# Seven half products for eight in the wide part of an in-projection, in two passes over pairs of token blocks

## The chip, the cores and the metric

One core of a Trainium2 chip. The metric is device time in microseconds (us) of one execution of the whole program; lower is better. TensorE (PE) multiplies, with its weight loads listed apart (PEld); VectorE (DVE), ScalarE (ACT) and GpSimd (POOL) do elementwise work; DMAs are issued from two queues, SyncE's (SP) and GpSimd's (POOL).

## The reference, cut to what matters

One layer on 2048 latent tokens (4 blocks of 512) and 256 context tokens, model width 1024, all in float32:

```python
h = rmsnorm(x, norm_g) * (1 + scale) + shift          # 2048 x 1024
ckv, kr, kb, vb, cq, za, qb, zb, ga, gb = split_cols(h @ w_in, ...)
q  = rmsnorm(cq, g_cq) @ w_uq                         # low-rank up-projections
kv = rmsnorm(ckv, g_ckv) @ w_ukv
oa = block_attention(q, k, v)                         # 8 heads, keys: latent and context
ob = neighborhood_attention(qb, kb, vb, ...)          # 8 heads
ya = (oa * silu(za)) @ w_oa;  yb = (ob * silu(zb)) @ w_ob
x  = x + gate * ((sigmoid(ga) * ya + sigmoid(gb) * yb) @ w_out)
out = rmsnorm(x, final_g)
```

The change is in `h @ w_in`, in the columns of qb, za, zb, ga and gb.

## The kernel before, in words

Every float32 product is made of three products of rounded parts: each operand is split into a high part (an ACT copy to the rounded type) and a low part (a DVE subtraction of that copy), and `mm3` multiplies high by high, high by low and low by high into one PSUM bank. So 128 columns of the in-projection (a chunk) for one token block are 8 k-tiles x 3 = 24 matmuls of 128x512 (`chunk`, PSUM tile accm).

Stage one (to about 216 us) computes h, block by block, and splits it into hh0..hh3 and hl0..hl3, 2 MB each, which stay in SBUF; beside it run the narrow columns (kv, q low-rank) and the context. Stage two is a list of items. Chunks 0 to 3 are the neighbourhood keys (evac_k), 4 to 7 its queries (evac_q), 8 to 15 the gates za and zb, 16 to 31 the gates ga and gb (evac_g: ACT sigmoid, for za and zb a DVE product, a store). Chunks 16 and 17 run as fillers elsewhere; the other 26 of chunks 4 to 31 are those that the change regroups. vb runs in two halves of 256 columns (`vb_run`: 16 token tiles x 24 matmuls, tile vacc) whose weights vhi and vlo have one buffer each in the pool vw.

Before each block of chunks 0 to 19, `pump(side_gen, 1)` takes one step of a side generator: first const_gen, then lowrank_gen, the up-projections. One of its steps is 3 matmuls for K (tile ka) or V (va), or 6 for q (qa), then `split_store`: ACT writes the high part into a tile sk or sq of the tag st (two buffers), DVE the low part, and POOL issues the stores to kmS or qm in DRAM (two stores for K and q, eight for the rope part of q, sqr). Its inputs (cnk, cnq) are loaded on SP's queue one block ahead. gate_gen (the output gate, tile pg) and presplit_gen (16 jobs that split w_o and w_out and store the parts) go beside the later chunks.

The attention follows in one loop: for a unit, 20 max matmuls (pm) with a DVE maximum each, a fold and a POOL spread, one matmul that puts the negated maximum in a row (pmf, copied by ACT into qh), then scores (S), exponentials (P) and outputs (oacc).

A scheduler decides from dependencies and priorities what order each engine's instructions stand in; each engine runs its own in order.

## Time and profile before

| | |
|---|---|
| median of 3 runs | 2533.22 us (2532.98 to 2537.31) |
| profiled execution, its own time | 2537.19 us |
| its span in the trace | 2535.4 us |
| TensorE busy | 2489.2 us, 98% |
| DVE, ACT, POOL busy | 1105.9, 903.1, 1093.5 us |
| mean granted clock of TensorE | 0.995 of full |

The span runs from the first to the last instruction of the trace. Busy shares are means over stages with different limits, so a change inside the in-projection has to be read from that stretch, 216 to 1055 us.

### The profile page before, as it was taken

Reading aid. Unit: us, or ns where it says so; the run is one execution under the profiler, and the core shown is the slowest. Engines: PE = TensorE matmul, PEld = TensorE weight load, DVE = VectorE, ACT = ScalarE, POOL = GpSimd, SP = SyncE. Lnnn points to the kernel's source line nnn. Section 1 sums busy time; section 2 is a strip of 40 time slices with the busy share of each in tenths; the row PEclk is TensorE's granted clock in tenths of the full one; section 3 lists DMA queues with packets and bytes.
Section 4 is the critical chain, followed back from the end, with each engine's and each line's share of the span. In section 5 each row is a group of like instructions: output and inputs, shape, how many; then the busy total and the mean of one; then the engine's idle time right before and its main releaser. Section 6 shows DMA issues by size and latency. Waiting matters only on the chain.

```text
span 2535.4 us, 34849 instructions
## 1 busy us (share of the span) xinstructions
PE 2489.2 (98%) x12796; PEld 1833.4 (72%) x12796; DVE 1105.9 (44%) x2285; ACT 903.1 (36%) x1774; POOL 1093.5 (43%) x861
## 2 busy tenths in 40 slices
PE   7999999999999999999999999999999999999998
PEld 4878888877789888756566656565656564888998
DVE  4654221222311211255465545465545446455654
ACT  4664432212322122234444444444444444112221
POOL 1312111111310000268877878777878886133220
PEclk9999999999999999999999999999999999999999
DMA  7535766456652466631415141514150333755542
GB/s 269 191 94 166 253 225 193 126 164 192 191 167 89 121 208 209 177 85 47 100 33 129 39 110 39 121 38 110 39 129 15 76 135 123 262 184 164 179 146 71
DMA packets 182979, 342.86 MB, mean 135 GB/s; under 512 B 25130, under 2 KB 95950, under 8 KB 175438
## 3 DMA queue, kind: packets, MB, share of 16 engines
q1 hardware_dynamic: 168872, 299.01, 39.5%
q0 software_dynamic: 13504, 41.35, 5.8%
q8 instruction: 100, 1.64, 0.3%
q14 instruction: 71, 0.58, 0.1%
q10 hardware_dynamic: 432, 0.28, 0.0%
HBM read 214.42 MB, written 126.13 MB: 134 GB/s over the span
## 4 chain that ended last, share of the span: by engine, by line
PE 89%; DMA 3%; DVE 3%; SPq 1%; ACT 1%; issue 1%; POOL 1%; POOLq 0%; DVEq 0%; ACTq 0%
PE accm L135 26%; PE S L807 15%; PE oacc L807 10%; PE pm L807 6%; PE f L135 5%; PE ya L135 4%; PE vacc L135 4%; PE nacc L226 3%; PE no L807 3%; PE accf L135 2%; PE accx L135 1%; PE nm L807 1%; DMA rz<-rzS 1%; PE pstl L185 1%; PE qa_False L135 1%
## 5 line engine op out<-in xcount | busy, mean ns | idle before, releaser
L1288 POOL TENSOR_TENSOR za<-za,P 128x1024 f32<-128x1024 f32 x217 | 516.3, 2379 | 111.2 <-ACT P L1278 107.5
L825 DVE TENSOR_REDUCE m<-pm 128x1 f32<-128x512 f32 (+1 forms) x640 | 388.1, 632 | 327.2 <-PE pm L807 320.6
L1278 ACT ACTIVATE P<-S 128x512 f32<-128x512 f32 x576 | 342.1, 596 | 452.4 <-PE S L807 432.7
L135 PE MATMUL accm<-hh,whi 128*128 128x512 f32 x928 | 366.8, 395 | 0.0
L135 PE MATMUL accm<-hl,whi 128*128 128x512 f32 x928 | 366.5, 395 | 0.0
L135 PE MATMUL accm<-hh,wlo 128*128 128x512 f32 x928 | 366.5, 395 | 0.0
L807 PE MATMUL oacc<-P,V 128*64 128x512 f32 x1152 | 286.7, 614 | 0.0
L807 PE MATMUL S<-qh,Kh 97*128 97x512 f32 x576 | 238.5, 414 | 3.9 <-DVE m L825 1.5
L807 PE MATMUL S<-ql,Kh 96*128 96x512 f32 x576 | 229.5, 398 | 0.0
L807 PE MATMUL pm<-Kh,qh 96*128 96x512 f32 (+1 forms) x640 | 223.5, 388 | 4.9 <-ACT P L1278 2.7
L807 PE MATMUL S<-qh,Kl 96*128 96x512 f32 x576 | 228.3, 396 | 0.0
L135 PEld LDWEIGHTS accm<-hh,whi 128*128 128x128 f32 x928 | 174.2, 188 | 42.8 <-issue 0.8
L135 PEld LDWEIGHTS accm<-hh,wlo 128*128 128x128 f32 x928 | 174.2, 188 | 42.4
L135 PEld LDWEIGHTS accm<-hl,whi 128*128 128x128 f32 x928 | 174.2, 188 | 41.4
L135 PE MATMUL ya<-u,woh 128*128 128x256 f32 x1024 | 185.0, 283 | 1.7 <-DVE t L1346 1.7
L807 PEld LDWEIGHTS pm<-Kh,qh 96*128 96x128 f32 x640 | 120.2, 188 | 90.5 <-issue 37.5
L807 PEld LDWEIGHTS oacc<-P,V 128*64 128x64 f32 x1152 | 69.5, 137 | 134.4 <-issue 133.6
L135 PE MATMUL f<-wfh,y 128*128 128x512 f32 (+1 forms) x528 | 161.6, 386 | 5.0 <-ACT y L1349 2.9
L135 PEld LDWEIGHTS ya<-u,woh 128*128 128x128 f32 x1024 | 160.1, 192 | 2.9 <-DVE t L1346 2.1
L135 PE MATMUL ya<-u,wol 128*128 128x256 f32 x512 | 144.9, 283 | 0.0
L807 PEld LDWEIGHTS S<-qh,Kh 97*128 97x128 f32 x576 | 109.4, 190 | 48.3 <-issue 16.9
L356 ACT ACTIVATE g<-accm 128x512 f32<-128x512 f32 x88 | 52.1, 592 | 249.5 <-PE accm L135 201.9
(1928 smaller groups left out, 4248.9 us busy)
## 6 DMA issues: line engine op xcount, KB each, us to landing
rawc<-in_wch SPq DMA_DIRECT2D x30, 512.0 KB
KA<-kB SPq DMA_DIRECT2D x16, 576.0 KB
xl<-in_xb SPq DMA_DIRECT2D x32, 256.0 KB
wm<-in_wmodb SPq DMA_DIRECT2D x8, 1024.0 KB
kmS<-sk POOLq DMA_DIRECT2D x32, 256.0 KB, 3.7
qR<-q SPq DMA_DIRECT2D x16, 512.0 KB
qm<-sq POOLq DMA_DIRECT2D x32, 256.0 KB, 3.9
woS<-ps SPq DMA_DIRECT2D x16, 512.0 KB
```

The lines of the kernel that those rows point to most:

```text
L135: nc.tensor.matmul(acc, a, b, start=(i == 0), stop=(i == n - 1))
L185: nc.tensor.matmul(pst[32 * j:32 * j + 32, :w], ones[:, 0:32], sq[:, :w], start=(kt < 4), stop=(kt >= 4))
L226: nc.tensor.matmul(acc[:, :n], a[:, k, sl], b[:, k, :n], start=(k == 0 and q == 0), stop=(k == KT - 1 and q == 2))
L356: nc.scalar.activation(s1, acc, AF.Sigmoid)
L807: ins = nc.tensor.matmul(*args, **kw)
L825: nc.vector.reduce_max(m5[:, qt, ci:ci + 1], pm[:, :b - a], axis=AX.X)
L1278: nc.scalar.activation(pt[:, x, :], sp, AF.Exp)
L1288: ve.tensor_tensor(za, za, pt, op=ALU.add)
```

## The change

26 wide chunks become 13 pairs. A pair (two column chunks), the two halves of the 1024 summed rows and two token blocks make a 2 x 2 x 2 block product, eight half products of 4 k-tiles x 3 = 12 matmuls; Strassen's scheme makes the same four outputs from seven products of sums of blocks. The first pass takes token blocks 0 and 1, the second 2 and 3. Per pass the sums of token halves (ta, tb) are made once (`token_sums`: POOL, DVE and ACT in 12 steps) and stand in the buffers of blocks 2 and 3 in the first pass; these blocks are kept in DRAM (hS) meanwhile and loaded again, into the buffers of 0 and 1, for the second. Per pair and pass two raw weight tiles are loaded, seven operands split (ACT, DVE), four sums made on POOL, and the products of 12 matmuls each accumulate in three banks A, B, C, with one ACT copy and five DVE additions between (c1, u2, u4). The up-projections stand alone between the passes; const_gen goes beside the K chunks; the two halves of vb follow the K chunks directly; gate_gen and presplit_gen go beside the pairs of the second pass, with a raw buffer of their own.

```diff
+        if c + 1 in (2, 3):
+            for a, t_ in enumerate((hh[c + 1], hl[c + 1])):
+                nc.gpsimd.dma_start(bc(hS[c - 1][a]), bc(t_))
...
-    def side_iter():
-        yield from const_gen()
-        yield from lowrank_gen()
...
-    items.insert(NSIDE, (lambda: vb_load(0), lambda wt: vb_run(0, wt)))
-    items.insert(NSIDE + 2, (lambda: vb_load(1), lambda wt: vb_run(1, wt)))
...
+        def k_run(wt, j=j):
+            chunk(f"m{j}", j, wt, lat[2:] + lat[1:2], evac_k)
+            pump(const_it, 1)
+        items.append((lambda j=j: load_chunk(j), k_run))
+    items += [(lambda hf=hf: vb_load(hf), lambda wt, hf=hf: vb_run(hf, wt)) for hf in range(2)]
...
+    def token_sums(ph, hp, hq, pl):
+
+        ta, tb_ = h_tiles(2, f"ta{ph}"), h_tiles(3, f"tb{ph}")
+
+        def split(src, dst, k, add=None):
+            nc.scalar.activation(dst[0][:, k, :], src, AF.Copy)
+            nc.vector.tensor_tensor(dst[1][:, k, :], src, bc(dst[0][:, k, :]), op=ALU.subtract)
...
+                nc.gpsimd.tensor_tensor(t1, q1_[0], p1_[0], op=ALU.subtract)
+                nc.vector.tensor_tensor(t2, q1_[1], p1_[1], op=ALU.subtract)
+                nc.vector.tensor_tensor(t1, t1, t2, op=ALU.add)
+                split(t1, ta, k)
+                nc.vector.tensor_tensor(t2, q2_[0], t1, op=ALU.subtract)
+                nc.vector.tensor_tensor(t2, t2, q2_[1], op=ALU.add)
+                split(t2, ta, k + HK)
+                yield
...
+            def operand(src, nm):
+                t = slot(nm)
+                f = t.rearrange("p k m -> p (k m)")
+                nc.scalar.activation(f[:, :W], src, AF.Copy)
+                nc.vector.tensor_tensor(f[:, W:], src, bc(f[:, :W]), op=ALU.subtract)
+                return [(t[:, k, :], t[:, HK + k, :]) for k in range(HK)]
...
+                nc.gpsimd.tensor_tensor(s1, a21, a22, op=ALU.add)
+                nc.gpsimd.tensor_tensor(s2, s1, a11, op=ALU.subtract)
+                yield operand(s2, f"w6{nm}")
...
+                A = bank(f"A{nm}")
+                run(0, A, True)
+                c1 = ct.tile([P, W], F32, tag="c1", name=f"c1{nm}", bufs=2)
+                nc.scalar.activation(c1, A, AF.Copy)
+                B = bank(f"B{nm}")
+                run(1, B, True)
+                u2 = ct.tile([P, W], F32, tag="u2", name=f"u2{nm}")
+                nc.vector.tensor_tensor(u2, B, c1, op=ALU.add)
+                C_ = bank(f"C{nm}")
+                run(2, C_, True)
+                run(3, B, False)
+                u4 = ct.tile([P, W], F32, tag="u4", name=f"u4{nm}")
+                nc.vector.tensor_tensor(u4, B, c1, op=ALU.add)
+                nc.vector.tensor_tensor(u4, C_, u4, op=ALU.add)
+                ev(jb, q, u4, W)
+                run(4, A, False)
+                ev(ja, p, A, W)
+                run(5, C_, False)
+                nc.vector.tensor_tensor(u2, C_, u2, op=ALU.add)
+                ev(jb, p, u2, W)
+                run(6, B, False)
+                nc.vector.tensor_tensor(c1, B, c1, op=ALU.add)
+                ev(ja, q, c1, W)
+                ops = nops
+                extra(es, i)
...
+    fast_columns(0, 0, 1, bops, raws, lambda es, i: None)
+
+    hp, hq = h_tiles(0, "2b"), h_tiles(1, "3b")
+    for c, t_ in ((0, hp), (1, hq)):
+        for x in range(2):
+            for a in range(2):
+                ks = slice(x * HK, (x + 1) * HK)
+                nc.sync.dma_start(bc(t_[a][:, ks, :]), bc(hS[c][a, :, ks, :]))
+    tg, bops = token_sums(1, hp, hq, tl)
+    for n, _ in enumerate(lowrank_gen()):
+        if n >= 24:
+            pump(tg, 1)
+    raws = load_pair(1, 0)
+    pump(tg, 99)
...
+    fast_columns(1, 2, 3, bops, raws, extra)
```

Three places in the order of instructions. The first is TensorE at the first up-projection step (ka0_0, va0_0). Before, it stands between two blocks of a chunk:

```order
L135 MATMUL accm1_2_2916<-hh2_1472,wlo1_2740 128x512
L135 MATMUL ka0_0_2951<-cnk0_2914,whkv_2910 128x512 x2
L135 MATMUL ka0_0_2951<-cnk0_2914,wlkv_2911 128x512
L135 MATMUL accm1_3_2960<-hh3_1850,whi1_2739 128x512
L135 MATMUL accm1_3_2960<-hl3_1851,whi1_2739 128x512
L135 MATMUL accm1_3_2960<-hh3_1850,wlo1_2740 128x512
```

After, it stands behind the last product of the first pass (B0_12: pass 0, pair 12), and the other steps follow it directly:

```order
L835 MATMUL B0_12_6045<-hl1_789,w30_12_6023 128x512
L835 MATMUL B0_12_6045<-hh1_788,w30_12_6023 128x512
L136 MATMUL ka0_0_6170<-cnk0_6166,whkv_6162 128x512 x2
L136 MATMUL ka0_0_6170<-cnk0_6166,wlkv_6163 128x512
L136 MATMUL va0_0_6179<-whkv_6162,cnk0_6166 128x512
L136 MATMUL va0_0_6179<-wlkv_6163,cnk0_6166 128x512
L136 MATMUL va0_0_6179<-whkv_6162,cnk0_6166 128x512
L136 MATMUL ka0_1_6186<-cnk0_6166,whkv_6162 128x512 x2
L136 MATMUL ka0_1_6186<-cnk0_6166,wlkv_6163 128x512
```

What moved: all 258 matmuls of the up-projections are one row now, in which only the 12 of A1_0's first product stand.

What ACT and SP have there in the changed kernel. On ACT (hhta1 and hhtb1 are high parts of the second pass's token sums, sk0_0 the first K copy, whkv the split of the K weights):

```order
L357 ACTIVATE g6_1_6135<-c10_12_6043 128x512
L117 ACTIVATE whkv_6162<-rawkv_6160 128x1024
L743 ACTIVATE hhta1_6153<-t11_0_6366 128x512
L743 ACTIVATE hhta1_6153<-t21_0_6367 128x512
L743 ACTIVATE hhtb1_6155<-t31_0_6388 128x512
L620 ACTIVATE sk0_0_6174<-ka0_0_6170 128x512
L743 ACTIVATE hhtb1_6155<-t41_0_6400 128x512
L652 ACTIVATE va0_0_6183<-va0_0_6179 128x512
L620 ACTIVATE sk0_1_6190<-ka0_1_6186 128x512
L652 ACTIVATE va0_1_6199<-va0_1_6195 128x512
```

On SP (gbS is the last gate store of the first pass, hh2b to hl3b the eight reloads, cnk0 the first up-projection input):

```order
L360 DMA gbS6_154<-g6_1_6135 128x512
L893 DMA hh2b_6141<-hS0_160 128x2048
L893 DMA hl2b_6142<-hS0_160 128x2048
L893 DMA hh3b_6143<-hS1_161 128x2048
L893 DMA hl3b_6144<-hS1_161 128x2048
L893 DMA hh3b_6143<-hS1_161 128x2048
L893 DMA hl3b_6144<-hS1_161 128x2048
L615 DMA cnk0_6166<-ckvS_70 128x2x512
L615 DMA cnk1_6168<-ckvS_70 128x2x512
```

The first K copy stands behind three copies of token sums, and its input behind the reloads on the queue.

The second place is POOL at the end of the up-projections (the last rope stores, then the first weight sums of pair 0 in the second pass, s11_0 to s21_0, whose split is operand w6):

```order
L625 DMA qm4_80<-sqr3_1_7007 16x2x512
L625 DMA qm5_81<-sqr3_1_7007 16x2x512
L625 DMA qm6_82<-sqr3_1_7007 16x2x512
L625 DMA qm7_83<-sqr3_1_7007 16x2x512
L818 TENSOR_TENSOR s11_0_7035<-raws1_5_7021 128x512
L822 TENSOR_TENSOR s31_0_7042<-raws1_4_7019,raws1_5_7021 128x512
L819 TENSOR_TENSOR s21_0_7036<-s11_0_7035,raws1_4_7019 128x512
```

The sums stand behind all 64 rope stores.

The third is TensorE at the end of the in-projection. Before, the first max matmuls of the attention stand inside chunk 23, seven chunks ahead of the end:

```order
L135 MATMUL accm23_2_7134<-hh2_1472,whi23_6604 128x512
L135 MATMUL accm23_2_7134<-hl2_1473,whi23_6604 128x512
L807 MATMUL pm0_0_0_8385<-Kh0_8342,qh0_8348 128x512
L807 MATMUL pm0_0_1_8388<-Kh0_8342,qh0_8348 128x512
L807 MATMUL pm0_0_2_8391<-Kh0_8342,qh0_8348 128x512
L135 MATMUL accm23_2_7134<-hh2_1472,wlo23_6605 128x512
L135 MATMUL accm23_2_7134<-hh2_1472,whi23_6604 128x512
L807 MATMUL pm0_0_3_8394<-Kh0_8342,qh0_8348 128x512
L135 MATMUL accm23_2_7134<-hl2_1473,whi23_6604 128x512
```

After, they stand behind the last product of the second pass (B1_12):

```order
L835 MATMUL B1_12_9031<-hl3b_6144,w31_12_9009 128x512
L835 MATMUL B1_12_9031<-hh3b_6143,w31_12_9009 128x512
L981 MATMUL pm0_0_0_9225<-Kh0_9182,qh0_9188 128x512
L981 MATMUL pm0_0_1_9228<-Kh0_9182,qh0_9188 128x512
L981 MATMUL pm0_0_2_9231<-Kh0_9182,qh0_9188 128x512
L981 MATMUL pm0_0_3_9234<-Kh0_9182,qh0_9188 128x512
L981 MATMUL pm0_0_4_9237<-Kh0_9182,qh0_9188 128x256
```

The 20 max matmuls, pmf0 and the first scores S0_0_0 now follow one another with no product between them.

## Rows read from the trace of the kernel before

**Rows 1.** Page, part 1: busy us, share of the span, instructions of each engine.
```profile
PE 2489.2 (98%) x12796; PEld 1833.4 (72%) x12796; DVE 1105.9 (44%) x2285; ACT 903.1 (36%) x1774; POOL 1093.5 (43%) x861
```

**Rows 2.** Page, part 4: the chain that ended last, by engine, by line.
```profile
PE 89%; DMA 3%; DVE 3%; SPq 1%; ACT 1%; issue 1%; POOL 1%; POOLq 0%; DVEq 0%; ACTq 0%
PE accm L135 26%; PE S L807 15%; PE oacc L807 10%; PE pm L807 6%; PE f L135 5%; PE ya L135 4%; PE vacc L135 4%; PE nacc L226 3%; PE no L807 3%; PE accf L135 2%; PE accx L135 1%; PE nm L807 1%; DMA rz<-rzS 1%; PE pstl L185 1%; PE qa_False L135 1%
```

**Rows 3.** The chain in order of time: start, us, what it is.
```profile
475.39 5.59 PE accm L135 x24
712.32 22.40 PE accm L135 x96
735.29 45.43 PE vacc L135 x384
```

**Rows 4.** Windows: length, busy PE, PEld, DVE, ACT, POOL, then clock, DMA share, GB/s.
```profile
300.00:400.00 100.00, 100.00 (x430) 80.46 (x429) 21.79 (x29) 33.40 (x57) 16.68 (x24) 1.00 0.68 220
900.00:1000.00 100.00, 100.00 (x431) 80.61 (x430) 17.00 (x22) 24.24 (x40) 0.00 (x0) 1.00 0.64 213
```

**Rows 5.** Windows again: the stretch that moved most.
```profile
10.00:20.00 10.00, 7.37 (x55) 2.95 (x54) 3.28 (x13) 7.02 (x11) 0.43 (x1) 1.00 1.01 401
```

**Rows 6.** Groups by form, DVE and ACT: busy us, mean ns, idle before.
```profile
L1347 DVE TENSOR_TENSOR t<-t 128x256 f32<-128x256 f32 x64 | 27.2, 425 | 1.9
L117 DVE TENSOR_TENSOR ps<-rawps,ps 128x512 fp32r<-128x512 f32 x32 | 21.5, 691 | 101.6 <-ACT ps L116 101.5
L1105 DVE TENSOR_TENSOR z<-z,rz 128x256 f32<-128x256 f32 x8 | 11.0, 1377 | 4.1 <-DMA rz<-rmS 3.7 <-issue 0.3
L617 ACT ACTIVATE sk<-ka 128x512 fp32r<-128x512 f32 x16 | 9.5, 592 | 5.7 <-DMA qR<-q 4.8 <-PE ka L135 0.5
```

**Rows 7.** Timeline of a K step, and a rope step's stores: start, us, what.
```profile
324.69 0.60 ACT L617 ACTIVATE sk<-ka 128x512 fp32r<-128x512 f32 x1 [0.15 <-PE ka L135]
325.33 0.69 DVE L618 SCALAR_TENSOR_TENSOR sk<-ka,sk 128x512 fp32r<-128x512 f32 x1
326.33 1.21 POOL L622 DMA_DIRECT2D kmS<-sk  x2 [3.89 <-DVE sk L618]
650.75 3.97 POOL L622 DMA_DIRECT2D qm<-sqr  x8 [3.01 <-DVE sqr L618]
```

**Rows 8.** DMA issues: count, KB each, us from issue to landing.
```profile
kmS<-sk POOLq DMA_DIRECT2D x32, 256.0 KB, 3.7
vaS<-va POOLq DMA_DIRECT2D x18, 256.0 KB, 4.8
qm<-sqr POOLq DMA_DIRECT2D x64, 64.0 KB, 3.7
```

**Rows 9.** Groups by form, POOL: DMA issues and one two-input operation.
```profile
L1184 POOL TENSOR_TENSOR za<-za 128x512 f32<-128x512 f32 x31 | 39.7, 1281 | 2.3
L622 POOL DMA_DIRECT2D qm<-sqr x64 | 31.8, 505 | 70.9 <-DVE sqr L618 68.8 <-issue 2.1
L622 POOL DMA_DIRECT2D kmS<-sk x40 | 24.2, 611 | 133.9 <-DVE sk L618 133.9
L622 POOL DMA_DIRECT2D qm<-sq x32 | 19.1, 602 | 100.4 <-DVE sq L618 100.4
L650 POOL DMA_DIRECT2D vaS<-va x18 | 15.8, 879 | 80.8 <-ACT va L649 69.5 <-ACT kb L337 5.7 <-issue 5.6
```

**Rows 10.** After an idle wait of TensorE: windows, and the timeline row before.
```profile
1103.60:1106.00 2.40, 2.33 (x5) 1.49 (x5) 0.69 (x1) 0.22 (x1) 2.01 (x3) 0.50 0.96 188
1106.00:1109.60 3.60, 3.60 (x9) 0.77 (x8) 0.69 (x1) 0.38 (x1) 2.35 (x1) 0.52 0.11 25
1103.67 0.79 PE L807 MATMUL nf<-nmd,onesr 128*128 128x512 f32 x1 [2.67 <-POOL nmd L812]
```

**Rows 11.** Start of the attention: timeline, and the maxima by tile pm.
```profile
1055.58 0.50 PE L807 MATMUL S<-qh,Kh 97*128 97x512 f32 x1 [0.69 <-ACT qh L834]
L825 DVE TENSOR_REDUCE m<-pm x40: 410/680/692, 861.7 to 1075.4; 128x1 f32<-128x512 f32 x32, 128x1 f32<-128x256 f32 x8
```

More of the change, by code (lines that the diff above doesn't have):

```diff
@@ L107, in tile_hybrid_layer @@
     gateS = scr("gateS", [1, D], F32)
+    hS = [scr(f"hS{i}", [2, P, KT, W]) for i in range(2)]
     def bc(ap):
@@ L395, in tile_hybrid_layer, with h_tiles @@
     env["q"] = nc.gpsimd
-    hh, hl, hes = [], [], ExitStack()
+    hh, hl, hes, hps = [], [], ExitStack(), []
+    def h_tiles(c, nm):
+        return [hps[c].tile([P, KT, W], F32R, tag=f"h{l}", name=f"h{l}{nm}") for l in "hl"]
     def open_h(c):
-        hp = pool(hes, f"hT{c}", side="right")
-        hh.append(hp.tile([P, KT, W], F32R, name=f"hh{c}"))
-        hl.append(hp.tile([P, KT, W], F32R, name=f"hl{c}"))
+        hps.append(pool(hes, f"hT{c}", side="right"))
+        hi, lo = h_tiles(c, f"{c}")
+        hh.append(hi)
+        hl.append(lo)
     def load_nat(k):
@@ L556, in tile_hybrid_layer @@
     xes = ExitStack()
-    def chunk_item(ci, j, evac, n=0):
-        sd = (lambda: pump(side_gen, n)) if n else None
-        srcs = lat[1:] if ci < 4 else lat
-        return (lambda: load_chunk(ci), lambda wt: chunk(f"m{ci}", j, wt, srcs, evac, sd))
     def const_gen():
@@ L691, in lowrank_gen @@
                         yield
+    tes, ves = ExitStack(), ExitStack()
+    tl = pool(tes, "tl")
+    const_it = const_gen()
     def vb_load(hf):
         if hf == 0:
-            pump(side_gen, 999)
-            env["vw"] = pool(xes, "vw")
+            pump(const_it, 999)
+            env["vw"] = pool(ves, "vw")
         vw = env["vw"]
@@ L703, in vb_run @@
     def vb_run(hf, wt):
[L704 removed]
+        for ti in list(range(8, 16)) + list(range(8)):
             vb_tile(ti, hh[ti // 4], hl[ti // 4], ti % 4, wt[0], wt[1], 2 * hf, 2)
[L707 to L711 removed]
     items = []
[L713 to L728 removed]
+    for j in range(4):
+        def k_run(wt, j=j):
[3 more added lines that the diff above has]
+    items += [(lambda hf=hf: vb_load(hf), lambda wt, hf=hf: vb_run(hf, wt)) for hf in range(2)]
     nxt = items[0][0]()
@@ new lines, in tile_hybrid_layer, with load_pair @@
+    pairs = []
+    for base, n, dst, silu in ((4, 4, None, 1), (8, 4, zaS, True), (12, 4, zbS, True),
+                               (16, 8, gaS, False), (24, 8, gbS, False)):
+        ev = evac_g(dst, silu) if dst is not None else evac_q
+        js = [j for j in range(n) if base + j not in (FILL, FILL + 1)]
+        pairs += [(base, js[i], js[i + 1], ev) for i in range(0, len(js), 2)]
+    def load_pair(ph, i):
+        base, a, b, _ = pairs[i]
+        return [raw_tile(I["wch"][base + j].rearrange("p k m -> p (k m)"), f"s{ph}_{base + j}").rearrange("p (x f) -> p x f", x=2)
+                for j in (a, b)]
@@ new lines, in tile_hybrid_layer @@
+    tg, bops = token_sums(0, (hh[0], hl[0]), (hh[1], hl[1]), tl)
+    raws = load_pair(0, 0)
+    pump(tg, 99)
+    ves.close()
+    fast_columns(0, 0, 1, bops, raws, lambda es, i: None)
[6 more added lines that the diff above has]
+    tg, bops = token_sums(1, hp, hq, tl)
@@ new lines, in tile_hybrid_layer, with extra, side_raw @@
+    for n, _ in enumerate(lowrank_gen()):
+        if n >= 24:
+            pump(tg, 1)
+    raws = load_pair(1, 0)
+    pump(tg, 99)
+    its = {}
+    def extra(es, i):
+        if i == 0:
+            xr = pool(es, "xr")
+            def side_raw(src, nm, n=KT * P):
+                t = xr.tile([P, KT * P], F32, tag="raw", name=f"raw{nm}")
+                nc.sync.dma_start(t[:, :n], src)
+                return t[:, :n]
+            its["g"], its["p"] = gate_gen(side_raw), presplit_gen(side_raw)
+        next(its["g"], None)
+        pump(its["p"], 2)
@@ L743, in tile_hybrid_layer @@
+    fast_columns(1, 2, 3, bops, raws, extra)
+    tes.close()
     hes.close()
```

96 lines of the change are left out of this document (75 added, 21 removed).

## The prediction

> **What bounds the kernel now.** I read the page first. TensorE is busy in 2489.2 of 2535.4 us, and the others are below half [rows 1]; the chain that ended last is 89% TensorE, its largest part, 26%, the wide chunks (accm) [rows 2]. So matmuls taken away are worth their full time only where nothing else then ends last. Next the chain in detail between 216 and 1055 us, where the in-projection runs: the reader sees whole chunks without a gap between them. 96 matmuls of 128x512 take 22.40 us, so one costs 22.40/96 = 0.2333 us; a half of vb is 384 matmuls of 256 columns in 45.43 us, 0.118 us each [rows 3]. Last the windows, for the room on the other engines: in 300 to 400 us, with the up-projections beside the chunks, DVE is busy 22%, ACT 33%, POOL 17%, and DMA works at 0.68; in 900 to 1000 us TensorE is busy 100.00 of 100 us as well [rows 4]. The stage is bound by TensorE, and its small units (258 up-projection matmuls, their splits and stores) cost nothing beyond their own matmuls, because each stands between two chunks of 24.
>
> **Removed.** 13 pairs x 2 passes x 7 products x 12 = 2184 matmuls stand for 26 x 4 x 24 = 2496: 312 fewer, 312 x 0.2333 = **-72.8 us**. All else is a cost.
>
> **Stage one.** Four stores of 2 MB to hS on POOL's queue, behind which the small stores of the context and nat tiles (two buffers) wait. At 401 GB/s, the most that a window shows [rows 5], 8.4 MB are 21 us of DMA, spread over stage one: +4, bounds 0 and 12.
>
> **Halves of vb.** The second half's weights use the buffers of the first, so their split begins after the last matmul of the first half: one split by ACT and DVE is 1.3 us [rows 6], the first two are needed before a matmul: +3, bounds 1.5 and 6.
>
> **Start of pass 0.** The second product waits for operand w6, whose ACT copy and DVE subtraction stand behind the last token sums. One sum step is up to three DVE operations of 128x512 at 0.69 us, two splits and one POOL operation of 1.28 us [rows 6, 9]. A DVE operation with two inputs in SBUF took 1377 ns for 128x256 where POOL was busy and 425 ns where it was not [rows 6], so the sums may take twice their bare time. I take +10, bounds 3 (hidden by vb) and 25 (all steps twice as long, not hidden).
>
> The Trainium skill (GPSIMD Engine Reference, the table of specifications) says that GpSimd shares its SBUF interfaces with VectorE, with contention when a DVE instruction has two SBUF inputs; the two rows just named agree, 1377 against 425 ns. By it, all sums at the slow row, this term would be 25 in place of 10.
>
> **The middle** is the largest term. Every up-projection group, before placed between chunks of 5.6 us [rows 3], now stands in one row after B0_12, the last product of pass 0. T is the end of that product. Up to T+21 SP's queue holds eight reloads of 1 MB, the last ones waiting for the last products, ahead of the first up-projection input (cnk0); some 6.3 MB remain after T, 16 us at 401 GB/s [rows 5], plus the wait for the first and the landing of the last. ACT's first up-projection copy also stands behind three splits of token sums, which need all reloads. So ka0_0 leaves at about T+25.
>
> Then a step is not paced by TensorE (3 matmuls, 0.7 us), but by its output tile st, of which there are two. One tile's round, read from one of them [rows 7]: ACT 0.60 from 324.69, DVE 0.69 until 326.02, POOL's two issues from 326.33, the second at 326.94, and its landing 3.7 after that [rows 8]: free at 330.6, a round of 6.0 us; with two tiles 3.05 us per step. 16 K steps of full width: 49; four context steps of half width at 2.5: 10. V steps use another tile, and ride along. Twelve token-sum steps, interleaved on ACT and DVE, about 0.8 each: +10. 16 nope steps of q, of the same form: 49. A rope step has eight issues, 3.97 us in all [rows 7]: 0.60 + 0.04 + 0.69 + 0.3 + the issues up to the last, 3.47, + 3.7 = 8.8, halved 4.4, by eight steps 35; the last landing is not waited for, -4. Behind the last issue POOL makes s1, s3, s2 for operand w6, two or three operations of 1.28 [rows 9] and a split of 1.3: +5.5. Together 25 + 49 + 10 + 10 + 49 + 35 - 4 + 5.5 = 180 us. TensorE's own work in it, 246 x 0.2333 + 12 x 0.118 + the first 24 matmuls of pair 0 (5.6) = 64, was in the kernel before too, so 116 us of it are new.
>
> From below: if landings were free, POOL's issues would pace the middle: 31.8 + 24.2 + 19.1 + 15.8 = 91 us [rows 9], plus 16 sums of 1.28 (20), plus the 25 at the start: 136, less 64 = 72. From above: landings at 4.8, as V's stores show [rows 8], make each round 1.1 longer, +22 over 40 steps, and the start may slip by 5: 145.
>
> After the idle time TensorE is slow at first. After a wait of 2.67 us at 1103.67 the granted clock was 0.50 and 0.52 in the next 6.0 us, the lower of the two levels (1.2 GHz in place of 2.4), in which 14 matmuls kept it busy for 5.93 us; at 0.2333 they are 3.3 [rows 10]: some 3 us lost each time. The middle: 116 + 3 = **+119**, bounds 72 and 148.
>
> The Trainium skill (DMA: Bandwidth & Descriptors, Anatomy of one DMA) gives about 2.0 us plus bytes/436e3 for a DMA issued by GpSimd: 2.6 us for 256 KB, where this trace shows 3.7. By it the rounds shorten by 1.1 (1.55 for the rope tiles), the middle by 26 us, and the sum falls by as much.
>
> **Inside the passes.** A pair is 84 x 0.2333 = 19.6 us of TensorE. DVE has at most 20 operations of 0.69 (7 subtractions of 128x512, 5 combinations, 4 products with the gate, 4 presplit subtractions): 13.8. ACT has 7 + 1 + 4 + 4 of 0.6, 10 to 12. POOL 4 x 1.28 = 5.1. All fit, if no more than a third of DVE's work is slowed by POOL. DMA in pass 1, by tile sizes: weights 1 MB, gate stores 1 MB, two presplit jobs 3 MB, a gate row 0.5: 5.5 MB in 19.6 us, 281 GB/s; a q pair, 7.5 MB, 383 GB/s, close to the 401 of [rows 5]. Raw tiles of the presplit have one buffer, off TensorE's path but for its eight small groups of the output gate: +8, bounds 0 and 40.
>
> **The end.** Before, the first 20 max matmuls of the attention (pm) and DVE's maxima over them lay inside chunk 23, 861 us; at 1055 the first S then waited 0.69 us for its row, and for nothing else [rows 11]. Now they stand right behind the last product, and Kh0's load (64 x 2304 in float32, its low half, qh, ql and krS's rows, by these sizes about 2 MB: 6 us and a landing) fills memory that this stage frees. The 20 maxima are 16 x 0.69 + 4 x 0.41 = 12.7 [rows 11]; the fold, the POOL spread, pmf and ACT's row come behind, 3.5; load and first matmul 5 exposed; less 4.7 of TensorE's own work in it, plus 3 for the clock: **+19**, bounds 14 and 25.
>
> **Sum.** -72.8 + 4 + 3 + 10 + 119 + 8 + 19 = +90, on the profiled execution's own time 2537.2: 2627. That lies 4.0 above the median of the three runs, 2533.2, so I predict **2623 us**. Under 0.2%, 5 us, a measurement here hardly tells a change from none.
>
> **Rivals.**
> A, faster: the middle hides. If its new idle time fell to 28 us or below, the sum would be zero or better; with none, -72.8 + 44 = -29, 2504. It needs up-projection and reloads within 92 us; POOL's issues alone take 91 [rows 9], and the reloads come first. For it: DMA and POOL have nothing else to do there. Chance 0.04.
> B: issues pace the middle, and landings overlap them: idle 72 in place of 116, 2579. For it: landings of 3.7 were read with DMA at 0.68 [rows 4, 8] and may be shorter alone. 0.20, and 0.03 more for a middle so short that the time is within 0.2% of before.
> C: pass 1 is bound by DMA or by DVE beside POOL: eight pairs at 25 us in place of 19.6 are +43 in place of 8: 2658. For it the 1377 ns of [rows 6]; against it, 281 GB/s against the 401 seen. 0.13.
> D: landings as the page on DMA has them: by the working above 2597. 0.10.
> The forecast has the rest, 0.50.
>
> The range: down to B with stage one, vb and the end at their lower bounds (2579 - 11), up to C with the upper bounds of the start (+15), of stage one, vb and the end (+17; 2658 + 32): 2568 to 2690. What is faster by over 0.2%: 0.04; within: 0.03; slower: 0.93.
>
> **What would show it.** The sum of TensorE's busy time falls by some 70 us, and its idle time, 46 us before, rises by 160. Almost all of it stands in one stretch, between B0_12 and B1_0, in which ACT's sk and sq wait for landings of kmS and qm, and POOL is the busiest engine with issues; a second gap of some 20 us stands between the last product and pmf, in which DVE is busy. In between, pairs should stand 19.6 us apart in both passes. I am wrong if up-projection steps come closer than 2.5 us (then B or A), if pairs of pass 1 stand 22 us or more apart (C), or if TensorE's clock stays low through the middle and beyond it.

## The result, and the profile after

The changed kernel takes 2720.4 us (median of four, 2718.1 to 2730.4), before 2534.4: a ratio of 1.0738, interval 1.0721 to 1.0755. That is slower by 186 us where 2623 and at most 2690 were forecast. The profiled execution took 2730.35 us, the longest of the four; its span is 2728.6, and all stage times of the changed kernel below are read from it.

From the page, part 1 (busy time) and part 4 (the chain by engine), against [rows 1] and [rows 2]:

```profile
PE 2490.8 (91%) x12484; PEld 1804.3 (66%) x12484; DVE 1375.4 (50%) x2659; ACT 1022.0 (37%) x1988; POOL 1270.6 (47%) x993
PE 50%; DMA 10%; DVE 5%; POOL 4%; issue 2%; ACT 2%; SPq 1%; POOLq 0%; ACTq 0%; DVEq 0%
```

TensorE's share of the chain falls from 89% to 50%. Its busy time is no smaller than before, 2490.8 against 2489.2, with 312 matmuls fewer: many of the rest run at the lower clock (mean granted clock 0.956 in place of 0.995). PE's longest waits between 200 and 1300 us (engine and tile, what it waited for; us in total, times, longest):

```profile
PE ka L136 <- ACT hhta L743: 23.8, 1, 23.8
PE B L835 <- ACT w L806: 23.4, 2, 13.5
PE ka L136 <- DVE sk L621: 23.1, 15, 3.0
PE qa_False L136 <- DVE sq L621: 22.2, 10, 5.7
PE pm L981 <- DMA Kh<-kmS: 14.8, 1, 14.8
PE B L835 <- DVE u L868: 14.2, 6, 3.1
PE A L835 <- ACT c L859: 12.3, 1, 12.3
PE qa_True L136 <- DVE rc L688: 11.0, 2, 6.6
PE C L835 <- DVE u L869: 9.3, 8, 2.6
```

They name the places: 23.8 is the reload ahead of the first up-projection step; the two waits B <- ACT w are the starts of the two passes (9.9 and 13.5); sk, sq and rc are the up-projections; Kh is the end; u, the combinations, are waits inside the passes. The stages by first and last start of their tiles, in us:

| stage | before | after | forecast | measured |
|---|---|---|---|---|
| 312 matmuls | | | -72.8 | -72.8 |
| first chunk (accm) starts | 245.4 | 259.7 | +4 | +14 |
| vb, 768 matmuls of 0.118 | 90.7 | 92.8 | +3 | +2 |
| pass 0, 254.8 of matmuls | | 419.5 to 697.4 | +10 | +23 |
| middle, 64 of matmuls | | 697.4 to 926.3 | +119 | +165 |
| pass 1, 249.2 of matmuls behind the middle | | 926.3 to 1209.5 | +8 | +34 |
| last product to the first S | 1.4 | 29.7 (4.7 of pm) | +19 | +24 |
| first S to the first ya | 1102.3 | 1112.3 | 0 | +10 |

The right column gives +199; the spans differ by 193, and the rest was not broken down. Every cost but that of vb came out above its forecast; the middle is 46 of the 109 us too few, pass 1 is 26.

The middle in windows (columns as in [rows 4]), with a stretch of each pass behind them:

```profile
700.00:720.00 20.00, 0.00 (x0) 0.00 (x0) 3.92 (x6) 0.63 (x1) 1.26 (x1) 0.56 1.00 406
740.00:760.00 20.00, 12.80 (x32) 7.70 (x33) 3.46 (x5) 6.13 (x12) 10.90 (x16) 0.74 0.87 225
820.00:840.00 20.00, 13.25 (x36) 9.19 (x36) 3.46 (x5) 2.99 (x5) 7.17 (x12) 0.69 0.69 194
880.00:900.00 20.00, 8.19 (x18) 5.27 (x18) 9.97 (x15) 6.62 (x11) 11.91 (x24) 0.59 0.54 134
540.00:560.00 20.00, 20.00 (x87) 16.14 (x86) 10.76 (x16) 7.24 (x12) 5.47 (x4) 1.00 0.33 112
980.00:1000.00 20.00, 18.28 (x78) 14.11 (x76) 12.51 (x18) 9.79 (x18) 5.04 (x4) 1.00 0.84 293
```

DMA is at 1.00 while the blocks are reloaded and at 0.80 to 0.89 with 225 to 237 GB/s from 720 to 780 us, beside K and V. From 780 us on, beside q, it is at 0.54 to 0.72 in all windows of 20 us but one (0.93): there the DMA engines are not full on average. TensorE, which waits again and again, has a mean clock of 0.59 to 0.91 in the windows from 720 us on. In the pass without side work, 540 to 560 is a stretch without a gap.

### The profile page after: what moved, and what is told of

The parts are those of the page before. It is cut to its first block, busy times and chain, and to the rows that moved or that the text cites. A ratio compares the mean times of both kernels' runs of the same rounds, so it can differ in the third digit from the quotient of the medians.

```text
span 2728.6 us, 35161 instructions
## 1 busy us (share of the span) xinstructions
PE 2490.8 (91%) x12484; PEld 1804.3 (66%) x12484; DVE 1375.4 (50%) x2659; ACT 1022.0 (37%) x1988; POOL 1270.6 (47%) x993
## 4 chain that ended last, share of the span: by engine, by line
PE 50%; DMA 10%; DVE 5%; POOL 4%; issue 2%; ACT 2%; SPq 1%; POOLq 0%; ACTq 0%; DVEq 0%
PE S L981 14%; PE oacc L981 9%; PE pm L981 5%; PE f L136 5%; PE ya L136 4%; PE no L981 3%; PE B L835 2%; PE C L835 2%; DMA kmS<-sk 1%; DMA qm<-sq 1%; DMA raws<-in_wch 1%; POOL qm L625 1%; PE nm L981 1%; PE A L835 1%; DVE m L999 1%
## 5 line engine op out<-in xcount | busy, mean ns | idle before, releaser
L818 POOL TENSOR_TENSOR s<-raws 128x512 f32<-128x512 f32 x26 | 36.3, 1396 | 289.2 <-DMA raws<-in_wch 275.0
L835 PE MATMUL B<-hhta,w 128*128 128x512 f32 x416 | 143.0, 405 | 24.5 <-ACT w L806 23.4
L835 PE MATMUL C<-hhtb,w 128*128 128x512 f32 x416 | 145.1, 410 | 9.3 <-DVE u L869 9.3
L981 PEld LDWEIGHTS S<-qh,Kl 96*128 96x128 f32 x576 | 110.5, 192 | 25.7
L807 DVE TENSOR_TENSOR w<-s,w 128x512 fp32r<-128x512 f32 x104 | 86.1, 839 | 81.8 <-ACT w L806 80.4
L806 ACT ACTIVATE w<-s 128x512 fp32r<-128x512 f32 x104 | 64.1, 629 | 162.3 <-POOL s L819 60.5
L981 PEld LDWEIGHTS S<-ql,Kh 96*128 96x128 f32 x576 | 110.8, 192 | 16.7 <-DMA ql<-qm 6.0
```

The source lines that it names most:

```text
L806: nc.scalar.activation(f[:, :W], src, AF.Copy)
L807: nc.vector.tensor_tensor(f[:, W:], src, bc(f[:, :W]), op=ALU.subtract)
L818: nc.gpsimd.tensor_tensor(s1, a21, a22, op=ALU.add)
L835: nc.tensor.matmul(acc, a, b, start=(first and n == 0), stop=(n == 3 * HK - 1), skip_group_check=True)
L981: ins = nc.tensor.matmul(*args, **kw)
```

## The experiments

Times are medians; before, in the same calls, was 2533.9 to 2539.2. The one-pass kernels ran four or five times, all others twice; as the four runs of the changed kernel alone lie between 2718.1 and 2730.4, a difference to it of under some 10 us says nothing. Middle: from the last product of pass 0 to the first product of pass 1 that needs token sums. Lines left out of a diff are marked with dots or told in angle brackets.

### The middle

**st6.** Six output tiles for two:

```diff
-                s1 = env["st"].tile([P, 2, W], F32R, tag="st", ...)
+                so = env["so"] = (env.get("so", -1) + 1) % 6
+                if so < 2: s1 = <the st tile>
+                else:      s1 = <weight tile whi or wlo of cw0 or cw1>
```

> The up-projections between the passes write their K and q outputs into six tiles in turn in place of two (the other four are weight tiles that are idle there); nothing else differs. Theory 1, rounds of two output tiles: the 229 us from the end of the last product of pass 0 to the second product of pair 0 in pass 1 shrink by 50 us or more, because K and V steps then go at POOL's issue pace (some 2.1 us per K and V together) and the nope steps of q at 1.2 to 1.5 us; the time falls from 2720 to about 2665. Theory 2, the DMAs are full there (share 0.87 to 0.89 in the K and V part): the landings only queue longer, the stretch shrinks by less than 15 us, and the time stays above 2705.

2688.5 us; the middle 193.7 in place of 228.9. Both theories hold in part: -32, less than the rounds' 50, more than a full DMA's 15. The tile view of sq (last line: from issue to landing, min/median/max), first of the changed kernel, then of this one:

```profile
DMA to landing us min/median/max: 3.0/4.0/7.1
```

```profile
DMA to landing us min/median/max: 3.5/7.0/10.6
```

With more tiles in flight the median landing takes 7.0 us in place of 4.0, so three times the tiles gave only part of the pace. The windows of this kernel in its K and V part and in its nope part of q show what is full then: DMA at 0.91 and 0.97, with POOL busy for little more than half:

```profile
740.00:780.00 40.00, 24.49 (x70) 15.72 (x69) 7.50 (x12) 11.89 (x23) 23.36 (x33) 0.71 0.91 260
807.00:843.00 36.00, 24.45 (x78) 17.65 (x78) 14.45 (x22) 10.73 (x18) 19.46 (x33) 0.76 0.97 337
```

**oneset.** No second token set: copies, reloads and sums are left out, and the second pass multiplies the operands of the first (another computation, for the time alone):

```diff
-                nc.gpsimd.dma_start(bc(hS[c - 1][a]), bc(t_))
...
-                nc.sync.dma_start(bc(t_[a][:, ks, :]), bc(hS[c][a, :, ks, :]))
-    tg, bops = token_sums(1, hp, hq, tl)
+    tg = iter(())
```

> Leaves out the second set of token operands: no copies of blocks 2 and 3 to DRAM, no reloads, no second token sums; the second pass multiplies the operands of the first, so blocks 2 and 3 of qb, za, zb, ga and gb come from the wrong tokens. Theory 1, this set costs stage one its 14 us (first chunk at 259.7 us in place of 245.4) and the middle its first 24 us and some 10 us of interleaved sums: the time falls by 45 to 50, to about 2672, and the first chunk starts near 246 again. Theory 2, the stores in stage one cost nothing and the late first chunk comes from something else (the earlier K chunks of other order): the first chunk stays near 259 and the time falls by 30 to 35.

2676.5 us, -44: first chunk at 243.0 (-17), middle 198.3 (-31). Theory 1 in the places, 1 us under its least fall of the time. Without reload and sums the up-projections alone still take 198 us.

**lr_vb.** All up-projections beside vb:

```diff
             vb_tile(ti, hh[ti // 4], hl[ti // 4], ti % 4, wt[0], wt[1], 2 * hf, 2)
+            pump(low_it, 2)
...
-    for n, _ in enumerate(lowrank_gen()):
-        if n >= 24:
-            pump(tg, 1)
```

> The 58 up-projection steps go beside the 32 tiles of vb, two per tile, in place of standing between the passes; between the passes only reloads, token sums and the first operands are left. Theory 1, the loss between the passes is that the steps' stores have nothing on TensorE beside them: the middle falls from 229 us to 35 to 45, the vb part rises from 92 to some 150 to 180 (58.8 us of matmuls more, and rounds of 3 us if the two output tiles still bind), and the time falls by 100 to 130, to about 2600. Theory 2, the reloads and token sums are what holds the middle, and the steps hide behind them: the middle stays above 100 us and the time falls by less than 50.

2695.4 us, -25: neither. The middle falls to 24.5, but chunks' end to pass 0 rises from 92.8 to 204.8 (the rope steps last 33 us longer than vb), pass 0 to 298.0 (its second product waits 29.9 us, since POOL makes the weight sums for it behind the last rope stores), and pass 1 to 325.9 (its first products wait for token sums one by one, with DVE busy in 32 of the 40 us from 853 to 893). The loss moves with the steps, and the token sums, 12 steps, need a cover of their own. The POOL rows at the start of pass 0:

```profile
552.06 10.90 POOL L627 DMA_DIRECT2D qm<-sqr  x22 [2.10 <-issue]
562.98 1.27 POOL L771 TENSOR_TENSOR t<-hh 128x512 f32<-128x512 f32 x1
564.20 1.26 POOL L822 TENSOR_TENSOR s<-raws 128x512 f32<-128x512 f32 x1
```

**mid.** st6, two rope tables, and reloads behind the first inputs:

```diff
+        if 8 <= n < 16:
+            c, x, a = (n - 8) // 4, (n - 8) // 2 % 2, n % 2
+            nc.sync.dma_start(bc((hp, hq)[c][a][:, ks, :]), bc(hS[c][a, :, ks, :]))
```

> The up-projections between the passes write into six tiles in turn in place of two, the rope tables have two tiles in place of one, and the reloads of blocks 2 and 3 are issued from the ninth step on, behind the first inputs of the up-projections. Theory 1, what stands between the passes is a chain of waits of its own (reload, then rounds of output tiles, then table loads): the first step follows the last product after 5 us in place of 24, the rope part shrinks further, and the stretch of 229 us falls to 140 to 165; the time is about 2640 to 2655. Theory 2, the stretch moves some 35 MB and DMA at 230 GB/s is its bound: early steps only slow down beside the reloads, the stretch stays near the 194 us that it had with six tiles alone, and the time at about 2688.

2679.6 us, the middle 188.6: nearer to theory 2. The first step comes after 8.6 us in place of 23.8, and from the first matmul of K to the first of q it takes 73 us in place of 63 (st6), beside the reloads. The windows of this kernel there:

```profile
700.00:720.00 20.00, 13.93 (x42) 8.88 (x40) 5.44 (x8) 6.93 (x12) 9.40 (x14) 0.76 1.02 415
720.00:740.00 20.00, 11.51 (x31) 6.38 (x31) 3.46 (x5) 5.99 (x11) 10.79 (x16) 0.76 1.02 327
```

**kv_vb.** K and V beside vb (four output tiles), q in the middle as in mid:

```diff
+            pump(kv_it, 2 if ti % 4 == 3 else 1)
...
+    for n, _ in enumerate(lowrank_gen("q")):
+        if 1 <= n < 9:
+            <one reload>
+        if n >= 10:
+            pump(tg, 1)
```

> The K and V up-projections (34 steps) go beside the 32 tiles of vb with four output tiles; between the passes only the 24 steps of q remain, with six output tiles, two rope tables, and reloads issued behind the first q inputs. Theory 1, the stretch between the passes is bound by the bytes that it moves: 49 MB in 229 us before, of which the K and V part is about 17; with some 32 MB left it takes 95 to 125 us, the vb part grows from 92 to 116 to 130 us, and the time falls to 2600 to 2640. Theory 2, it is bound by reload and token sums, one behind the other, whatever stands beside them: the stretch stays at 150 us or more and the time at 2670 or more.

2661.4 us, -59: the middle 134.4, chunks' end to pass 0 127.5. Theory 1 in direction, the middle 9 to 39 us over its size: 32.7 MB are left, with DMA at 0.98 to 0.99 from 735 to 795 us. Behind that DMA is at about a half, and first DVE is full (28.7 of 30 us at 795 to 825, token sums and the rope part of q), then POOL (27.6 of 30 us at 820 to 850, rope stores). So what is full in this stretch changes twice. Against mid the middle falls by 54 us and the vb part grows by 35, and the time falls by 18. This was the fastest form with two passes.

### Stage one

**store_vb.** The copies to hS written into the first half of vb:

```diff
+            if hf == 0 and ti in (9, 10, 11, 12):
+                c, a = (ti - 9) // 2, (ti - 9) % 2
+                nc.gpsimd.dma_start(bc(hS[c][a]), bc((hh, hl)[a][c + 2]))
```

> The four copies of blocks 2 and 3 to DRAM move from stage one to the first half of vb, on the same queue; nothing else differs. Theory 1, their 8.4 MB hold stage one up by 14 to 17 us and would be hidden where DMA works at 0.15 to 0.2: the first chunk starts near 243 to 246 in place of 259.7, the vb part keeps its 92 us, and the time falls by 12 to 17, to about 2705. Theory 2, the loss only moves, because the token sums that overwrite these blocks then wait for the copies: the first product of pass 0 that needs sums is as late as before, and the time is the same.

2720.1 us, but nothing was tested: the trace has the copies at 152 to 198 us again, since the scheduler took them as soon as the blocks were there. First chunk at 252.6; across these kernels it starts between 252.6 and 260.9 wherever the copies are in stage one.

**store_late.** Held back by a data dependence:

```diff
+                t_ = (hh[2], hl[2], hh[3], hl[3])[ti]
+                nc.vector.tensor_copy(t_[0:1, 0, 0:1], bc(t_[0:1, 0, 0:1]))
+                nc.gpsimd.dma_start(bc(hS[ti // 2][ti % 2]), bc(t_))
```

> The four copies of blocks 2 and 3 to DRAM are held back until the first half of vb by a one-element rewrite of each tile, on which the copy depends (the earlier attempt was moved back to its old place by the scheduler). Theory 1, in stage one these 8.4 MB delay the loads of x for the next block, which run beside them: the waits of the sums of squares (pstl) there vanish, the first chunk starts at 243 to 247 us in place of 253 to 260, and the time falls by 8 to 15, to about 2707. Theory 2, the loss only moves: the token sums of pass 0 wait for the copies, and the time is the same.

2721.6 us. First chunk at 245.6, as before the change: the copies were what held stage one up (in the changed kernel xl's loads are late there: ACT waits for them 13.8 us in all, 5.8 at most, and PE 4.6 us for the sums of squares behind them; the rest of the delay was not followed). But the time is the same, theory 2, though not by the token sums: vb takes 102.3 in place of 92.8, so of the 14 us some 5 are left at the start of pass 0, less than the runs differ by. vb's longest waits are

```profile
PE vacc L136 <- ACT v L384: 7.3, 2, 5.5
```

behind vb's own small stores, which now run beside the copies.

### The passes

**dup.** The first product of each pair twice, 312 matmuls:

```diff
+                product(A, ops[0], bops[0], True)
                 run(0, A, True)
```

> The first of the seven products of each pair is multiplied twice (the second time over the first), so both passes have again the 2496 matmuls of before: 312 more, 72.8 us at 0.2333 us each. Theory 1, the passes are bound by TensorE for the most part: the first pass grows by its full 36.4 us, the second by 10 to 36 (its waits for raw weights take up some of it), the time by 50 to 73, to 2770 to 2793. Theory 2, the passes are paced by the other engines: the time grows by less than 25.

2784.4 us, +64: pass 0 +31, pass 1 +27. Theory 1: the matmuls taken away are worth 58 to 64 of 72.8 us in the passes, not lost there.

**side_p0.** Gate and output-weight splits beside pass 0 (`extra` handed to the first call in place of the second):

```diff
-    fast_columns(0, 0, 1, bops, raws, lambda es, i: None)
+    fast_columns(0, 0, 1, bops, raws, extra)
...
-    fast_columns(1, 2, 3, bops, raws, extra)
+    fast_columns(1, 2, 3, bops, raws, lambda es, i: None)
```

> The output gate's loads and the 16 splits of the output weights go beside the pairs of the first pass in place of the second; nothing else differs. Theory 1, the second pass is slow (283 us for 1068 matmuls that need 249) because raw weight loads stand on SP's queue behind these stores and loads: the second pass falls by some 25 to 30 us, the first pass rises by the same kind of wait, 10 to 30, since its queue then holds them, so the time moves by less than 20 either way. Theory 2, the second pass is slow for reasons of its own (token operands, waits for the combinations): it stays above 275 us and the first pass stays at 278, and the time is the same.

2722.0 us: pass 1 257.2 (-26), pass 0 306.7 (+29). Theory 1: the 26 us are the side work's.

**spread.** A step behind each product, not all at a pair's end:

```diff
             raw = raw_tile(src, f"ps{q}")
+            yield
             for n in range(2):
+                yield
...
                     product(acc, ops[m], bops[m], first)
+                    extra(es, i * 7 + m)
```

> In the second pass the splits of the output weights and the output gate are taken in small steps, one behind each product, in place of all of a pair's at its end, with a step between each load, each split and the next; nothing else differs. Theory 1, weight loads are late because they stand on SP's queue behind stores that wait for a split: spread out, they come in time, the second pass falls from 283 us to 255 to 265 and the time by 20 to 28. Theory 2, the second pass is slowed by the amount of DMA (5.5 MB per pair): it stays above 275 us and the time is the same.

2729.9 us, pass 1 290.3: my cure failed, so this does not show that bytes are the bound either. SP still waits as long behind the split; its waits between 926 and 1215 us, first of the changed kernel, then of this one:

```profile
SPq L598 <- DVE ps L118: 67.7, 26, 9.1
```

```profile
SPq L601 <- DVE ps L118: 70.9, 23, 11.8
```

**raw2.** Raw weights a pair ahead (the side work also begins two pairs later, and its loads use another idle tile):

```diff
+        if ph == 1 and i % 2:
+            <raw tiles of their own, in place of cw's>
...
+                        cur, ahead = ahead, load_pair(ph, i + 2) if i + 2 < len(pairs) else None
+                        g = prep(i + 1, *cur)
...
+        if i < 2:
+            return
```

> In the second pass the raw weights of every other pair have tiles of their own and are loaded a pair earlier; the side loads use a tile that is idle after the queries, and begin with the third pair. Theory 1, the second pass waits because a pair's raw weights are asked for only when the last pair's tiles are free, and land late beside the side traffic: with a pair's lead the second pass falls from 283 us to 255 to 265, and the time by 18 to 28, to about 2697. Theory 2, the operands are late for other reasons (splits of the side work on ACT and DVE ahead of them): the second pass stays above 275 us.

2706.2 us, -14, pass 1 270.2 (-13): about half of the excess of 26, between the two theories; whether the lead or the later start of the side work gives it, this run does not tell. The chain that the lead is to break is, in the changed kernel, SP behind a split, raws late, POOL's s1 waiting (135 us in all), w late on ACT and DVE, and DVE's combination u behind w in the same queue, for which PE waits. One such wait (start, us, what):

```profile
994.27 1.29 POOL L818 TENSOR_TENSOR s<-raws 128x512 f32<-128x512 f32 x1 [18.53 <-DMA raws<-in_wch]
998.76 2.41 DVE L807 TENSOR_TENSOR w<-s,w 128x512 fp32r<-128x512 f32 x2 [0.15 <-ACT w L806]
1001.09 0.68 DVE L868 TENSOR_TENSOR u<-B,c 128x512 f32<-128x512 f32 x1
1001.83 0.50 PE L835 MATMUL B<-hh3b,w 128*128 128x512 f32 x1 [2.88 <-DVE u L868]
```

The other half stays open.

**all3.** store_late, kv_vb and raw2 together.

> The three edits together: late copies, K and V beside vb with q between the passes, and raw weights a pair ahead. If the terms are independent, the time is that of the K and V run less 8 to 15 and less 18 to 28: about 2580 to 2600, still above the 2534 of before, because the end (some 34 us with the slow start of the attention), the rest of the middle (some 50) and the start of pass 0 (some 20) remain. If the copies beside vb and the K and V stores get in one another's way, it is 2610 or more.

2668.4 us, 7 more than kv_vb alone: what raw2 gives is lost where the copies, K and V stores and vb's stores meet (chunks' end to pass 0 is 160.6, against 127.5). The terms are not independent.

### One pass alone

**half** and **half_plain**:

```diff
+                for c in (2, 3):                      # 26 chunks, blocks 2 and 3, eight products
+                    pump(side_gen, 4 - c)
+                    chunk(f"m{ci}", j, wt, [lat[c]], ev)
...
+    vb_run(0, nxt, range(8, 16))
+    vb_run(1, vb_load(1, 1), list(range(8, 16)) + list(range(8)))
+    vb_run(0, vb_load(2, 0), range(8))
...
+    del pairs[-2:]
+    fast_columns(0, 0, 1, bops, raws, lambda es, i: None)   # half_plain: chunks over lat[:2]
```

> One pass alone: token blocks 2 and 3 are multiplied with eight products as before, with the up-projections beside them; then K, vb (its first half's weights loaded twice, so that its tiles of blocks 0 and 1 come last), the token sums of blocks 0 and 1 over the buffers of 2 and 3, and eleven pairs with seven products; the last two pairs of blocks 0 and 1 have eight products, so that the attention's first maxima fit in beside them. No copies to DRAM, no reloads, no stretch between passes. 132 matmuls fewer are -30.8 us. Theory 1, the loss came from the second pass: left are the start of the pass (10 or less), two or three short waits in it with the low clock behind them (6) and a third load of vb weights (3): the time is 2515 to 2527, under the 2534 of before. Theory 2, the scheme itself costs what it saves, in operands and combinations: 2534 or more.

> The same order with eight products in place of seven in the one pass (no token sums, no operands or combinations): 132 matmuls more than the kernel with one pass. Theory 1: it takes 2534 to 2542, the time of before and a few us for the reordering, and the kernel with seven products is 15 to 25 us faster than it. Theory 2: it is as fast as the kernel with seven products or faster, and what is gained or lost there is the reordering's.

2579.8 us (a ratio of 1.0172 to the kernel before, interval 1.0152 to 1.0191) and 2591.4 (1.0218, 1.0194 to 1.0242). Neither theory: the scheme gains 12 us, and the order, with eight products, costs 56. Both wait 24 to 27 us near 600 us for a weight split (accm <- ACT whi) behind the bunch of side loads, half also 8.3 at the third vb weights. The start of the pass costs 2.5 us here, covered by vb, and the attention starts as in the kernel before.

**half2** and **half2_plain**, with an order that was to remove these waits:

```diff
+        env["n"] = 2 if i < 9 else 1
         run_(cur)
+        if i < 9:
+            next(gate_it, None)
+        elif i < 25:
+            pump(pre_it, 1)
...
+    chunk("m28b", 4, w4, lat[:2], evac_g(gbS, False))
+    vb_run(0, vt, range(8))
```

> The one-pass kernel with its waits mended: one split of output weights per chunk from the tenth on in place of two per chunk at the end, the output gate beside the first nine chunks, and one plain chunk of blocks 0 and 1 between the second and third set of vb weights. Theory 1, the 45 us of waits in the first form were the side work's: the gaps of 24, 5, 3 and 8 us and the low clock behind them go, the time falls by 40 to 50, to 2530 to 2540, no longer clearly slower than before and perhaps a few us faster. Theory 2, the work beside the shorter chunks (11.2 us per weight load in place of 22.4) is too dense whatever its order: new waits take their place and the time stays above 2555.

> The same with eight products throughout, no token sums, operands or combinations. Theory 1: the 132 matmuls more cost 30.8 us less the waits inside the pass with seven products (some 8 to 15): it is 15 to 25 us slower than the kernel with seven, 2550 to 2562. Theory 2: the difference stays at the 12 us of the first pair of kernels, since these waits are the scheme's own.

2580.0 us (1.0181, 1.0157 to 1.0204) and 2596.5 (1.0244, 1.0221 to 1.0267). The old gaps went and others came, theory 2 for the order. PE's waits in half2 between 240 and 720 us:

```profile
PE accm L136 <- ACT whi L117: 17.5, 1, 17.5
PE qa_True L136 <- ACT whqTrue L117: 6.6, 1, 6.6
PE ka L136 <- ACT va L649: 6.1, 1, 6.1
PE accm L136 <- ACT g L357: 5.2, 1, 5.2
PE ka L136 <- ACT whkv L117: 4.1, 1, 4.1
```

The scheme's gain in this pair is 16.5 us of 30.8, in theory 1's range for half2_plain; but the runs of each kernel differ by 13 us, so it is not told apart from the 12 of the first pair. No kernel here beats the one before.

## Why the prediction was wrong

The direction, the places and their order were right: the saving is there (dup), the gap between B0_12 and B1_0 is the largest cost, ka0_0 came 23.8 us after the last product (25 forecast), and the end has its gap with DVE's 20 maxima behind Kh0's load. The size was not. Nor did TensorE's busy time fall by 70 us: in the middle its mean clock was 0.71; from 931 us to the end of pass 1 it was full but for three stretches of 3.4 us.

**The step that failed** is the round of an output tile, "a round of 6.0 us; with two tiles 3.05 us per step", and for rope 4.4. Counted by ACT's copies, with which a round begins, a K step of full width took 4.0 us (723.3 to 783.3), a nope step of q 4.0 (808.6 to 872.0) and a rope step 6.2 (872.0 to 921.8). Over 16, 16 and 8 steps these are some 45 us, about the 46 by which the middle was too small. Two of the three have the landing for a reason, the third has not.

*K.* The round took landings of 3.7 us from a stretch in which one step came per chunk [rows 7, 8], with DMA at 0.68 [rows 4]. In the middle the steps, their inputs and the reloads come back to back: some 49 MB by the windows (the GB/s of the eleven 20-us windows from 700 to 920 add up to 2452). DMA was no term of the sum there; from above I let V's 4.8 stand for it. Measured, in the DMA view of 720 to 796 us:

```profile
kmS<-sk POOLq DMA_DIRECT2D x32, 256.0 KB, 4.8
vaS<-va POOLq DMA_DIRECT2D x16, 256.0 KB, 5.6
```

*Nope.* The median landing of 4.0 hides two groups: of the 32 stores 18 landed after 3.0 to 4.3 us and 13 after 6.4 to 7.1, the latter while the inputs of the next block (cnq) came in. The DMA views of 811 to 820 us and, last, of 819 to 826:

```profile
qm<-sq POOLq DMA_DIRECT2D x4, 256.0 KB, 6.6
cnq_False<-cqS SPq DMA_DIRECT2D x2, 512.0 KB
qm<-sq POOLq DMA_DIRECT2D x4, 256.0 KB, 3.7
```

*Rope.* Its stores landed after 2.5 us in the median, sooner than the 3.7 of the sum. It was slow for a reason that I had read past: its table ropeT has one tile, so each block waits for a load that is asked for when the last block is done. DVE's waits for it are 8.0, 3.9 and 4.1 us; the first:

```profile
881.33 0.69 DVE L688 TENSOR_TENSOR rc<-qa_True,ropeT 128x512 f32<-128x512 f32 x1 [7.96 <-DMA ropeT<-in_ropeT]
882.07 1.22 PE L136 MATMUL qa_True<-cnq_True,whqTrue 128*128 128x512 f32 x2 [6.64 <-DVE rc L688]
```

No run shows the table's share by itself: the rope stores are issued within 48 us here, 40 with six output tiles and one table (st6) and 39 with two tables (mid), where POOL's issues alone are 32.

st6 shows that the two tiles were part of the pace (35 of 165 us), mid that lifting the chain of waits alone gives little more, and kv_vb that fewer bytes and steps there shorten the middle most, though most of that returns beside vb. Rival B (issues pace the middle, landings overlap) did not come: POOL was busy in 112 of the 229 us, and the landings of K and of some of the nope stores were longer, not shorter. Its lower bound of 72 us for the idle time lay far off; even without reload and sums (oneset) the middle is 198 us.

The Trainium skill (DMA: Bandwidth & Descriptors, Anatomy of one DMA) gives, by its fit of 2.0 us and the bytes by 436e3, an estimate of 2.6 us for a store of 256 KB. The trace differs, 4.8 for K here and 7.0 for q with six tiles; the estimate for one DMA did not hold here for stores that stand in a queue beside other traffic.

**Inside the passes**, "All fit" failed for pass 1: there was room on DVE and DMA (DVE 0.56 to 0.68, DMA 209 to 300 GB/s between 940 and 1040 against 281), but the order in SP's queue and in DVE's turned late weights into waits of PE, eleven in the pass, 17 us in all. The sign that the prediction had set for rival C came: nine pairs stood 21.5 to 25.1 us apart, seven of them 22 or more. C gave +43 by an engine that is full; +34 came with none full, by late weights in the waits named, and the rest, the lower clock at the start and after waits among it, was not broken down. side_p0 shows whose they are, raw2 half of how. DVE beside POOL, C's other half, has a part in it: the row of 1377 ns [rows 6] is a mean of four operations that lay over one of POOL's and took 2.0 to 2.6 us and four that did not, at 0.4, and the same split is found in pass 1 (last section).

**The start** of pass 0 was within its bounds (23 of 25): 9.9 us at B0_0, waits of 3.1 and 3.0 later and the clock behind them. half shows that vb's last tiles can cover it (2.5). **Stage one** exceeded its bound of 12 by a little (+14; +7 to +15.5 over the kernels with copies in it), and through other traffic than I named: in part the loads of xl. **The end** was 24 of 19, right; that the attention's first two units then run slower (+10) was missed: PE waits 5.7 us for ql there, with DMA at 1.02 to 1.03 from 1220 to 1260, and the clock is low until 1245.

The range of the time failed because its top, 2690, took the upper bounds of the smaller terms and left out that of the middle, 148 for 119: with these 29 us it would have been 2719. (That bound has a slip of 2 us in it: 116 + 22 + 5 is 143, not 145.) And the middle's bounds themselves came from rows of a stretch in which one step came per chunk. Five of the six costs came out above their value; queues that other work had kept half empty before are seen behind the middle and pass 1, and a reason that all five share is not shown.

## What to carry to other kernels

Seven products for eight save an eighth of a stage's matmuls, and that pays only if operands, sums and copies have matmuls to hide behind; here one pass returned 12 to 16 of 31 us, and every form that made room for it lost more. Before moving small steps out from between large ones, add up the bytes that they move and divide by the stretch that is left: a landing read where one store goes at a time is no price for a landing in a queue beside loads. And look at what stands behind a store on the issuing queue: a store that waits for a split held back the weight loads that the next matmuls needed here. And carry the upper bound of the largest term into the range.

## What the hardware showed that was not expected

- The same store landed sooner or later with what else was in flight: sq stores of 256 KB landed after 3.0 to 4.3 us (18 of 32) and, beside loads of 512 KB, after 6.4 to 7.1 (13 of 32) with two output tiles; with six tiles and DMA at 0.97 the median was 7.0, the longest 10.6.
- Some of the 2 to 3 us waits inside a pass bring a stretch of the lower clock with them: windows of 20 us at 1000 to 1020 and 1080 to 1100 show a granted clock of 0.91, with waits of 2.9 and 2.1 us in them, while the windows at 1040 to 1060 and 1160 to 1180 stay at 1.00 with waits of 2.5 and 2.6.
- DVE's subtraction of 128x512 took 884 ns on average in pass 1 where its input was POOL's fresh sum:

```profile
L807 DVE TENSOR_TENSOR w<-s,w 128x512 fp32r<-128x512 f32 x52 | 45.4, 884 | 48.5 <-ACT w L806 47.6
L807 DVE TENSOR_TENSOR w<-raws,w 128x512 fp32r<-128x512 f32 x36 | 26.5, 735 | 15.5 <-ACT w L806 15.3
```

The mean mixes two kinds. By the starts and ends in the trace, 16 of these subtractions overlap an operation of POOL and took 1228 ns on average (0.68 to 1.84 us), and 35 overlap none and took 687, as before the change (691 [rows 6]).
